# A two-layer streaming encoder step: plain products in the first two SwiGLU pairs, x on a second queue, padded attention tiles, earlier output weights, one root chain

## The chip, the cores and the metric

The kernel runs on one core of a Trainium2 chip. The core has five engines that run side by side, each with its own instruction queue: TensorE (PE, matmuls; its weight loads are listed as PEld), VectorE (DVE), ScalarE (ACT), GpSimd (POOL) and SyncE (SP, which here only issues DMAs). The metric is the device time of one execution in microseconds, as the median of several runs.

## What is computed

560 columns (512 frames of a prompt, 32 frames of a running stream, 16 meta tokens) of width 1024 pass through two layers. Each layer is a half-step SwiGLU, a mixer, and a second half-step SwiGLU; the first layer's mixer is a gated linear attention (GLA), the second's a latent attention (MLA).

```python
def swiglu_half(h, norm_w, w_gate, w_up, w_down):
    hn = rmsnorm(h, norm_w)
    return h + 0.5 * ((jax.nn.silu(hn @ w_gate) * (hn @ w_up)) @ w_down)
...
for i in range(DEPTH):
    hp = swiglu_half(hp, ffn1_norm[i], ...)      # hs (the sample) alike
    xp = rmsnorm(hp, mix_norm[i])
    if i % N_MIXERS == 0: dp, sp = gla_mixer(xp, ...)
    else:                 dp, cp, rp = mla_mixer(xp, ...)
    hp = hp + dp
    hp = swiglu_half(hp, ffn2_norm[i], ...)
y_prompt = rmsnorm(hp[:, N_META:], final_norm)
```

In MLA the score of a query and a key is a product over 128 latent channels (folded into the keys' side by the kernel) plus one over 64 rotary channels.

## The kernel before

**Numbers in two parts.** Every matmul operand is kept as a high part in a reduced-precision 4-byte format and a low part, the rest: `split` (L377) makes the high part by a cast on ACT (L378) and the low part by a subtraction on DVE (L379). A product of two numbers is three matmuls: high by high (L419), weight's low by high (L420), weight's high by low (L422). `mm` (L411) writes these for a list of operand tiles.

**The state.** `h` holds the residual stream, 8 tiles of 128 rows by 560 columns, in two halves of 280 columns.

**A SwiGLU** (`ffn`, L576) takes its 22 gate-and-up tiles in pairs. One pair is a 2 x 2 block product (two tiles, two halves of the input rows, two halves of the columns), and `gate_up` (L476) does it with seven products in place of eight, after Strassen and Winograd. Its operands are b11 and b21 (the first column half, rows 0 to 511 and 512 to 1023, scaled by the norm's weight), b22, and the combinations t4 to t7; its weights are the blocks q0 to q3 and sums of them (`Weights`, L283, with DVE additions at L298). Each of the seven products is 24 matmuls of 280 columns into one of the double banks A, B and C. Between the products `gap` issues pieces of the previous group's down projection (`down`, L558, banks Y) as filling. Weights come by DMA on SP's queue (`quadrant`, L395; L399), the high and low parts of a block by `whole` (L401).

**The norm's factor** is not applied to the operands but after the product: squares are summed over the tiles (`square`), a matmul with ones sums over the rows (L451, three columns for three pieces of a half), DVE refines the inverse root in a chain of small steps (`rsqrt`, L463; L465 to L473), and three transposes spread the result over a bank (L458), from where it is copied to `yn`. One such chain is `roots(half)` (L443); in the first pair of a SwiGLU the first half's chain begins after product t6 and the second half's after t5.

**The start.** For the first SwiGLU the operands are made in the pair itself (`lazy`, `make`, L239): b11 and b21 first, then t6, t5, t7, t4 and b22, each when its product is due, with x arriving by DMAs that alternate with those of the first weights on SP's queue (L1362, L1378, L1381). In the later ones the operands are made piece by piece while the projection before them adds to `h` (`Quads.parts`, L187), and the first weights are loaded and summed at the same place (`ahead`).

**GLA** ends with `wout` (L663): the output projection of two heads at a time. With the second pair of heads each piece is followed by the operands of the next SwiGLU; the four weights are loaded one by one when their first piece is due (L667 to L670), on SP's queue, and split on ACT and DVE.

**MLA** (`attention`, L1072): for eight heads and four blocks of 128 queries, `scores` (L1241) makes three matmuls with the keys, one with the high part of the rotary keys over 128 rows (queries' high and low part stacked, L1254) and one with their low part over 64 rows (L1255). For odd heads the queries' parts lie the other way round. `weigh` (L1281) sums five blocks of values, the last of 64 rows. `sample` (L1118) does the running stream, whose 288 keys fill two blocks of 128 and one of 32 rows. `wout` (L1297) is the output projection, with the next SwiGLU's operands behind each piece as in GLA and its weights loaded one by one.

A scheduler orders the instructions of each engine from this program; each engine then runs its own list in order.

Of the kernel before, what the change touches and what calls it, by code (L numbers as in the profile page):

```python
# [18 lines left out]
P = 128  # L19
# [115 lines left out]
class Quads(Normed):  # L135
# [6 lines left out]
    SETS = (("b11", "b21"), ("t5",), ("t6", "b22", "t7", "t4"))  # L142
# [3 lines left out]
    def __init__(self, net, name, halves, pool, tmp, raws):  # L146
# [5 lines left out]
        self.lazy, self.early, self.finish = False, [], {}  # L152
# [14 lines left out]
    def operand(self, op):  # L167

        if self.lazy and op not in self.made:
            self.make(op)  # L170
        return [self.place(op, i) for i in range(4)]
# [7 lines left out]
    def scaled_parts(self, op, i, m):  # L179

        nc = self.net.nc
        hi, lo = self.place(op, i)
        h, w = self.piece(m, 0), self.weight(m)
        nc.scalar.activation(hi, h, AF.Copy, scale=w)
        nc.vector.scalar_tensor_tensor(lo, h, w, hi.bitcast(F32), op0=ALU.mult, op1=ALU.subtract)

    def parts(self, m, hf):  # L187
# [3 lines left out]
        if hf == 0:  # L191
            self.scaled_parts("b11" if m < 4 else "b21", i, m)
# [6 lines left out]
        else:  # L199
            b12, t5 = self.kept.pop(i)  # L200
            q = self.tmp.tile([P, 4, 280], F32, name="q", tag="q", bufs=1)
            t6, b22, t7, t4 = (q[:, j, :n] for j in range(4))
# [36 lines left out]
    def make(self, op):  # L239
# [3 lines left out]
        t = self.tmp  # L243
        if op in ("b11", "b21"):
            for i in range(4):
                self.scaled_parts(op, i, i + 4 * (op == "b21"))
        for i in range(4):
            b12, t5, b22, t6 = (t[4 * j + i][:, :n] for j in range(4)) if t else (None,) * 4
            if op == "t6":
                nc.scalar.activation(b12, self.piece(i, 1), AF.Copy, scale=self.weight(i))  # L250
                v.scalar_tensor_tensor(t5, self.piece(i, 0), self.weight(i), b12, op0=ALU.mult, op1=ALU.subtract)
                nc.scalar.activation(b22, self.piece(4 + i, 1), AF.Copy, scale=self.weight(4 + i))
                v.scalar_tensor_tensor(t6, t5, -1.0, b22, op0=ALU.mult, op1=ALU.subtract)
                net.split(*self.place("t6", i), t6)
            elif op == "t5":
                net.split(*self.place("t5", i), t5)
            elif op == "t7":
                v.tensor_tensor(b12, b22, b12, op=ALU.subtract)
                net.split(*self.place("t7", i), b12)
            elif op == "t4":  # L260
                v.scalar_tensor_tensor(t6, self.piece(4 + i, 0), self.weight(4 + i), t6, op0=ALU.mult, op1=ALU.add)
                net.split(*self.place("t4", i), t6)
            elif op == "b22":
                net.split(*self.place("b22", i), b22)
        self.made.add(op)

    def roots(self, hf):

        c0, c1 = self.halves[hf]
        if self.lazy:  # L270
            for m in range(ND):
                Normed.square(self, hf)
        self.finish[hf] = self.net.roots(hf, c1 - c0, D)
# [63 lines left out]
class Net:  # L337
    def __init__(self, ctx, tc, a):
# [12 lines left out]
        nc.vector.memset(self.ones, 1.0)  # L351
        self.accs = {}
# [48 lines left out]
    def whole(self, src):  # L401
        hi = self.w.tile([P, 8, P], F32R, name="whi", tag="whi")
        lo = self.w.tile([P, 8, P], F32R, name="wlo", tag="wlo")
        self.split(*(t.rearrange("p a b -> p (a b)") for t in (hi, lo)), src)
# [57 lines left out]

    def rsqrt(self, y, s, vh, t, dim):  # L463
# [3 lines left out]
        for _ in range(3):  # L467
            if y.shape[-1] > 3:
# [7 lines left out]
    def gate_up(self, i, l, f, xs, act, tp, between):  # L476
# [6 lines left out]
        if left is None:  # L483
            left = Weights(self, i, l, f, xs.raws)
            for q in (0, 1):
                left.load(q)
                if xs.early:
                    xs.early.pop(0)()
# [3 lines left out]
        def product(to, op, more=False):  # L492
            if xs.lazy and op in ("b11", "b21"):
                w, x = next(left), xs.operand(op)
            else:
                x, w = xs.operand(op), next(left)
# [40 lines left out]
        if first:  # L537
            xs.roots(0)
# [1051 lines left out]
```

## Time and profile before

| | |
|---|---|
| time, median of 3 runs | 2082.53 us (2082.26 to 2088.39) |
| the profiled execution | 2092.07 us, span 2090.3 us |
| mean granted TensorE clock | 0.984 |
| PE busy | 2029.9 us, 97% of the span, 15290 matmuls |
| DVE busy | 1637.7 us, 78% |
| ACT busy | 1018.8 us, 49% |
| DMA queue of SP and ACT | 173.09 MB, 26.1% of 16 engines' span |

Busy time is the time in which an engine executes instructions; waiting is not counted. Since matmuls overlap, a busy PE may still run slowly: what counts there is the distance from the start of one matmul to the start of the next, and the granted clock (PEclk, 1.00 is full speed). A row of the timeline gives the start, the length, the engine, the source line, the operation with output and input tiles, and in brackets how long the engine had been idle and what released it.

### The profile page before, as it was taken

How to read it: one execution, taken by the hardware profiler on the slowest of the kernel's cores; microseconds unless marked ns; L12 is line 12 of the kernel's file. 1: busy time of each engine (PE TensorE's matmuls, PEld its weight loads, DVE VectorE, ACT ScalarE, POOL GpSimd, SP SyncE). 2: the span in 40 equal slices, each digit the busy share in tenths (PEclk: the TensorE clock that was granted, in tenths of full speed). 3: DMA queues.
4: the chain of work that ended last, by engine and by line, in shares of the span. 5: the costliest groups of instructions: out<-in, count | busy, mean ns of one | idle time of the engine just before them, and what ended most of it. 6: DMA issues, size and time to landing. Idle time of an engine off the chain costs nothing.

```text
span 2090.3 us, 38017 instructions
## 1 busy us (share of the span) xinstructions
PE 2029.9 (97%) x15290; PEld 1985.0 (95%) x15290; DVE 1637.7 (78%) x3097; ACT 1018.8 (49%) x1822; POOL 51.3 (2%) x117
## 2 busy tenths in 40 slices
PE   5999999999998999999999999999999999999997
PEld 5999999989998999999999999999988899999997
DVE  7887879656657987878888878796787898877884
ACT  6444445445535544444455444454575565444451
POOL 0000000101110000000000000000110000000000
PEclk8999999999999999999999999999999999999998
DMA  3233231212222223233312232323111313333221
GB/s 132 87 101 101 83 110 61 96 66 72 66 81 73 65 96 106 83 107 104 101 55 93 86 106 89 101 69 105 60 55 43 126 46 97 101 97 102 86 77 58
DMA packets 91905, 180.16 MB, mean 86 GB/s; under 512 B 10240, under 2 KB 21888, under 8 KB 91728
## 3 DMA queue, kind: packets, MB, share of 16 engines
q1 hardware_dynamic: 87904, 173.09, 26.1%
q10 hardware_dynamic: 3824, 4.63, 0.7%
q8 instruction: 120, 1.97, 0.4%
q14 instruction: 57, 0.47, 0.1%
HBM read 173.69 MB, written 3.99 MB: 85 GB/s over the span
## 4 chain that ended last, share of the span: by engine, by line
PE 81%; DVE 10%; DMA 3%; ACT 2%; issue 2%; SPq 0%; POOL 0%; DVEq 0%; ACTq 0%; POOLq 0%
PE Y L422 8%; PE Y L419 8%; PE Y L420 8%; PE A L420 5%; PE A L422 5%; PE A L419 5%; PE ps L419 3%; PE C L420 3%; PE B L420 3%; PE C L419 3%; PE B L419 3%; PE B L422 3%; PE C L422 3%; PE ps L422 3%; PE ps L420 3%; DVE wlo L379 3%
## 5 line engine op out<-in xcount | busy, mean ns | idle before, releaser
L419 PE MATMUL Y<-ah,whi 128*128 128x280 f32 (+1 forms) x1408 | 376.1, 293 | 6.2 <-ACT ah L378 4.2
L379 DVE TENSOR_TENSOR wlo<-fr,whi 128x1024 fp32r<-128x1024 f32 x308 | 372.0, 1217 | 9.0 <-ACT whi L378 8.6
L420 PE MATMUL Y<-ah,wlo 128*128 128x280 f32 (+1 forms) x1408 | 375.4, 293 | 0.0
L378 ACT CAST whi<-fr 128x1024 fp32r<-128x1024 f32 x308 | 320.5, 1049 | 96.9 <-PE C L422 37.5
L419 PE MATMUL A<-x,whi 128*128 128x280 f32 (+1 forms) x1056 | 283.8, 294 | 16.1 <-ACT whi L378 16.1
L420 PE MATMUL A<-x,wlo 128*128 128x280 f32 (+1 forms) x1056 | 283.4, 294 | 1.0 <-DVE wlo L379 1.0
L419 PEld LDWEIGHTS Y<-ah,whi 128*128 128x128 f32 x1408 | 266.7, 189 | 8.1 <-ACT ah L378 5.1
L570 DVE SCALAR_TENSOR_TENSOR h<-Y,h 128x280 f32<-128x280 f32 (+1 forms) x320 | 140.9, 443 | 162.4 <-PE Y L422 161.7
L420 PEld LDWEIGHTS Y<-ah,wlo 128*128 128x128 f32 x1408 | 266.9, 190 | 0.0
L379 DVE TENSOR_TENSOR wlo<-raw,whi 128x512 fp32r<-128x512 f32 (+5 forms) x231 | 196.0, 850 | 77.6 <-ACT whi L378 72.8
L378 ACT CAST whi<-raw 128x512 fp32r<-128x512 f32 (+5 forms) x231 | 169.8, 736 | 163.4 <-PE ps L422 48.5
L422 PE MATMUL Y<-al,whi 128*128 128x280 f32 (+1 forms) x1408 | 234.4, 292 | 0.0
L298 DVE TENSOR_TENSOR fr<-fr 128x1024 f32<-128x1024 f32 x176 | 214.4, 1218 | 20.5 <-DMA fr<-W 18.7
L419 PEld LDWEIGHTS A<-x,whi 128*128 128x128 f32 x1056 | 201.5, 191 | 16.8 <-ACT whi L378 16.5
L420 PEld LDWEIGHTS A<-x,wlo 128*128 128x128 f32 x1056 | 201.7, 191 | 1.4 <-DVE wlo L379 1.4
L422 PEld LDWEIGHTS Y<-al,whi 128*128 128x128 f32 x1408 | 201.9, 190 | 0.0
L420 PE MATMUL C<-x,wlo 128*128 128x280 f32 (+1 forms) x704 | 189.2, 294 | 3.5 <-DVE wlo L379 3.5
L419 PE MATMUL C<-x,whi 128*128 128x280 f32 (+1 forms) x704 | 189.3, 293 | 0.6 <-ACT whi L378 0.6
L419 PE MATMUL B<-x,whi 128*128 128x280 f32 (+1 forms) x704 | 188.2, 292 | 0.7 <-ACT whi L378 0.7
L420 PE MATMUL B<-x,wlo 128*128 128x280 f32 (+1 forms) x704 | 187.9, 293 | 0.6 <-DVE wlo L379 0.5
L422 PE MATMUL A<-x,whi 128*128 128x280 f32 (+1 forms) x1056 | 180.8, 293 | 0.0
L506 ACT COPY r<-A 128x560 f32<-128x560 f32 (+1 forms) x132 | 82.3, 623 | 171.3 <-PE A L422 170.1
(368 smaller groups left out, 4071.6 us busy)
## 6 DMA issues: line engine op xcount, KB each, us to landing
fr<-W SPq DMA_DIRECT2D x352, 256.0 KB, 3.4
raw<-W SPq DMA_DIRECT2D x80, 512.0 KB, 3.5
raw<-W SPq DMA_DIRECT2D x100, 256.0 KB, 3.0
raw<-W SPq DMA_DIRECT2D x40, 128.0 KB, 2.0
h<-xT SPq DMA_DIRECT2D x3, 560.0 KB, 7.5
raw<-W SPq DMA_DIRECT2D x4, 384.0 KB, 3.1
o_y<-h SPq DMA_DIRECT2D x8, 136.0 KB, 2.7
o_y<-h ACTq DMA_DIRECT2D x8, 136.0 KB, 2.4
```

The source lines that it names most:

```text
L298: self.net.nc.vector.tensor_tensor(r[out], r[x], r[y], op=ALU.add)
L378: self.nc.scalar.copy(hi, src)
L379: self.nc.vector.tensor_tensor(lo, src, hi.bitcast(F32), op=ALU.subtract)
L419: f(hi[:, b0 + k, :], xh[:, c], start=not more and k == 0, stop=False)
L420: f(lo[:, b0 + k, :], xh[:, c], start=False, stop=False)
L422: f(hi[:, b0 + k, :], xl[:, c], start=False, stop=k == n - 1)
L506: nc.scalar.copy(r[:, :, :n], of[:, :, :n])
L570: nc.vector.scalar_tensor_tensor(self.h[:, m, c], Y[:, :n], 0.5, self.h[:, m, c], op0=ALU.mult, op1=ALU.add)
```

## The change

1. **First SwiGLU, first two pairs.** `plain_gate_up` takes the place of `gate_up`: eight plain products with the operands b11, b21, b12 and b22 and the weights q0 to q3, no sums of blocks. The first pair makes its operands as they are due (`direct`) and copies its results out until the norm's factor is there; the second pair makes the combined operands for the later pairs in four of its gaps (`combine`). From the third pair on `gate_up` goes on as before.
2. **Loads.** The norm weights and the first column half of x are issued on ACT's queue; SP's begins with the first weight block. The first weight is split in two halves. A one-column Silu on ones stands ahead of the x loads on ACT, and eleven matmuls on ones (128 x 128) stand ahead of the first product on PE.
3. **One root chain** (`roots2`) for both halves, six columns wide, in the first pair of every SwiGLU, after product t6 (in the first SwiGLU, after the fourth plain product).
4. **Padding in MLA.** The low parts of the rotary keys, the last block of values and of the weights on it, and the third block of the sample's past get zero rows up to 128; the queries' parts lie the same way for all heads.
5. **Early weights.** The four weights of the last output projection of GLA and of MLA are loaded before its first piece.

```diff
+    def plain_gate_up(self, i, l, f, xs, act, tp, between):
...
+        def product(to, q, op, more=False):
+            if early and not more:
+                x = xs.direct(op)
+            if q not in w:
+                w[q] = self.whole(W.r[q], 2 if early and q == 0 else 1)
+            if not early or more:
+                x = xs.direct(op)
+            for j in range(2):
+                self.mm(to[:, j, :n], w[q], 4 * j, x, (0, n), more)
+            if early and q < 2:
+                for _ in range(4):
+                    Normed.square(xs, op[-1] == "2")
...
+        def gap():
+            done[0] += 1
+            if not early and done[0] <= 4:
+                xs.combine(done[0] - 1)
+            if done[0] < 8:
+                between(done[0])
...
+        for (j, hf), bank, tag in zip(((0, 0), (0, 1), (1, 0), (1, 1)), "ACBA", ("ra", "rb", None, None)):
+            D = self.bank2(bank)
+            for kh in (0, 1):
+                product(D, 2 * j + kh, ("b11", "b21", "b12", "b22")[2 * hf + kh], kh == 1)
+                if kh == 0:
+                    gap()
+            held.append((j, hf, hold(D, tag) if tag else D))
+            if early and (j, hf) == (0, 1):
+                xs.roots()
...
     def gate_up(self, i, l, f, xs, act, tp, between):
...
         if first:
-            xs.roots(0)
+            xs.roots()
...
             finish(0, 0, C, r1, ALU.add)
-            xs.roots(1)
...
             def wout(g):
...
+                if g == 1:
+                    for b in (0, 2, 1, 3):
+                        L[b] = self.load(("go", g, b))
...
         def scores(h, t):
...
-                pe.matmul(o, qr[hi, qc], rpl[hi, kc], start=False, stop=True)
+                pe.matmul(o, qr[:, qc], rpl[:, kc], start=False, stop=True)
...
         def weigh(h):
...
-            self.mm3(O[:, 384:512], (vh[:64, 4, hc], vl[:64, 4, hc]), (eh, el), False, False)
+            self.mm3(O[:, 384:512], (vh[:, 4, hc], vl[:, 4, hc]), ee, False, False)
...
                     if heads[-1] == MH - 1:
+                        for b in (0, 2, 1, 3):
+                            W[b] = self.load(("mo", heads[0], b))
                         gone.close()
                         after.append(turn())
...
-    nc.sync.dma_start(net.nv, a["nv"])
+    nc.scalar.dma_start(net.nv, a["nv"])
...
-        nc.sync.dma_start(net.h[:, k0:k1, c0:c1], a["xT"][:, k0:k1, c0:c1])
-
-    x0.lazy = True
-    x0.early = [lambda: x_in(4, 8, 0), lambda: (x_in(0, 4, 1), x_in(4, 8, 1), nc.sync.dma_start(net.ident, a["ident"]))]
+        (nc.scalar if hf == 0 else nc.sync).dma_start(net.h[:, k0:k1, c0:c1], a["xT"][:, k0:k1, c0:c1])
+
+    x0.plain = 2
+    x0.first = Weights(net, 1, 0, 0, x0.raws)
+    x0.first.load(0)
     x_in(0, 2, 0)
     x_in(2, 4, 0)
+    x_in(4, 8, 0)
+    x0.first.load(1)
+    x_in(0, 4, 1)
+    x_in(4, 8, 1)
+    x0.first.load(2, 3)
...
+    warm = net.bank("Y")
+    for _ in range(11):
+        nc.tensor.matmul(warm[:, :P], net.ones, net.ones, start=True, stop=True)
```

ScalarE at the program's start, before (h is the residual stream that x is loaded into, nv the norm weights, fr a weight block as it arrives, whi its high part, x the operands' parts):

```order
L184 ACT_TABLE_LOAD [waits DMAHW1_49]
L184 ACTIVATE x_114<-h_64,nv_65 128x280 [waits DMAHW0_49]
L184 ACTIVATE x_115<-h_64,nv_65 128x280
L184 ACTIVATE x_116<-h_64,nv_65 128x280 [waits DMAHW2_49]
L378 CAST whi_110<-fr_99 128x1024 [waits DMAHW4_49,DMAHW3_49]
L184 ACTIVATE x_117<-h_64,nv_65 128x280
L436 ACTIVATE acc_262<-h_64 128x280
```

The same place on ScalarE, now:

```order
L1459 DMA nv_65<-nv 128x67
L344 ACT_TABLE_LOAD
L344 ACTIVATE silu_69<-ones_67 128x1 [waits DVE_49]
L1475 DMA h_64<-xT 128x2x280 x2
L1475 DMA h_64<-xT 128x4x280 [waits DMAHW0_49]
L181 ACTIVATE x_130<-h_64,nv_65 128x280 [waits DMAHW4_49]
L181 ACTIVATE x_131<-h_64,nv_65 128x280
L181 ACTIVATE x_132<-h_64,nv_65 128x280 [waits DMAHW6_49]
L181 ACTIVATE x_133<-h_64,nv_65 128x280
L371 CAST whi_151<-fr_78 128x512 [waits DMAHW1_49]
L371 CAST whi_151<-fr_78 128x512 [waits DMAHW2_49]
```

The table load now waits for no DMA and stands ahead of the x loads, which ACT itself issues; the weight's cast has become two of half the width, both behind the four operands.

VectorE in GLA's output projection, before (raw is an output weight as it arrives, wlo a weight's low part, q the combined operands of the next SwiGLU, acc its sums of squares, ps the bank of a piece):

```order
L206 SCALAR_TENSOR_TENSOR q_7775<-h_64,nv_65,q_7775 128x280 [waits DVE_49]
L223 TENSOR_TENSOR acc_7676<-acc_7676,sq2_7782 128x280 [waits Activation_49]
L223 TENSOR_TENSOR acc_7678<-acc_7678,sq2_7782 128x280
L379 TENSOR_TENSOR wlo_7796<-raw_7794,whi_7795 128x1024 [waits DMAHW4_49]
L379 TENSOR_TENSOR x_7614<-q_7775,x_7614 128x1120 [waits Activation_49]
L379 TENSOR_TENSOR wlo_7818<-raw_7816,whi_7817 128x1024 [waits DMAHW5_49]
```

The same operands of the next SwiGLU on VectorE, now:

```order
L203 SCALAR_TENSOR_TENSOR q_7782<-h_64,nv_65,q_7782 128x280 [waits DVE_49]
L220 TENSOR_TENSOR acc_7683<-acc_7683,sq2_7789 128x280 [waits Activation_49]
L220 TENSOR_TENSOR acc_7685<-acc_7685,sq2_7789 128x280
L372 TENSOR_TENSOR wlo_7798<-fr_7636,whi_7797 128x1024 [waits DMAHW5_49,DMAHW4_49]
L372 TENSOR_TENSOR x_7627<-q_7782,x_7627 128x1120 [waits Activation_49]
L760 TENSOR_TENSOR h_64<-ps_7801,h_64 128x280 [waits PE_49]
```

The two low parts from raw have left this place (they now stand ahead of the projection, among the last head's rows); that from fr, a weight of the next SwiGLU, stands here now.

TensorE in the first pair of the SwiGLU behind GLA, before (ident and ry are the transposes of the inverse roots, ones and acc the sums that begin a chain):

```order
L422 MATMUL B_8088<-x_7612,whi_8089 128x280
L458 MATMUL Y_8121<-ident_66,ry_8074 128x128 [waits DVE_49]
L458 MATMUL Y_8121<-ident_66,ry_8074 128x128 x2
L451 MATMUL Y_8131<-ones_67,acc_7678 128x1 [waits PE_49]
L451 MATMUL Y_8131<-ones_67,acc_7678 128x1 x2
L419 MATMUL A_7988<-x_7613,whi_8149 128x280 [waits Activation_49]
```

The same place on TensorE, now:

```order
L418 MATMUL A_7983<-x_7629,whi_8129 128x280
L475 MATMUL Y_8119<-ident_66,ry2_8072 128x128 [waits DVE_49]
L475 MATMUL Y_8119<-ident_66,ry2_8072 128x128 x2
L475 MATMUL Y_8161<-ident_66,ry2_8072 128x128 [waits PE_49]
L475 MATMUL Y_8161<-ident_66,ry2_8072 128x128 x2
L415 MATMUL C_8171<-x_7626,whi_8172 128x280
```

Both halves' transposes now follow one another, one product later than the first half's did, and the sums of the second half have moved up to those of the first.

More of the change, by code (lines that the diff above doesn't have):

```diff
@@ L151, in __init__ @@
         self.sets, self.kept, self.made = None, {}, set()
-        self.lazy, self.early, self.finish = False, [], {}
+        self.plain, self.finish = 0, {}
     def place(self, op, i):
@@ L237, in __call__, with direct, combine @@
             self.first.sums()
-    def make(self, op):
+    def direct(self, op):
+        m0, hf = {"b11": (0, 0), "b21": (4, 0), "b12": (0, 1), "b22": (4, 1)}[op]
+        pairs = [(t[:, 0, :self.n], t[:, 1, :self.n]) for t in self.extra] if op == "b12" else self.operand(op)
+        if op not in self.made:
+            self.made.add(op)
+            for i, (hi, lo) in enumerate(pairs):
+                self.scaled_parts(hi, lo, m0 + i, hf)
+        return pairs
+    def combine(self, i):
         net, nc, n = self.net, self.net.nc, self.n
@@ L242, in make @@
         v = nc.vector
[L243 to L273, printed above, removed]
+        f, g, q = self.tmp[i % 2], self.tmp[2], self.tmp[3]
+        b12, b22, t5, t4, t6, t7 = f[:, 0, :n], f[:, 1, :n], g[:, 0, :n], g[:, 1, :n], q[:, 0, :n], q[:, 1, :n]
+        for x, m in ((b12, i), (b22, 4 + i)):
+            nc.scalar.activation(x, self.piece(m, 1), AF.Copy, scale=self.weight(m))
@@ L461, in roots, with roots2, finish @@
         return finish
+    def roots2(self, n, dim):
+        pe = self.nc.tensor
+        s = self.bank("s")
+        first = (0, P, n - P)
+        for hf in (0, 1):
+            for j, c in enumerate(first):
+                k = 3 * hf + j
+                pe.matmul(s[:, k:k + 1], self.accs[hf][:, c:c + P], self.ones[:, :1], start=True, stop=True)
+        y, vh, t = (self.np_.tile([P, 6], F32, name=x, tag=x) for x in ("ry2", "rv2", "rt2"))
+        self.rsqrt(y, s[:, :6], vh, t, dim)
+        def finish(hf):
+            out = self.bank("s")
+            for j in (2, 0, 1):
+                k = 3 * hf + j
+                pe.transpose(out[:, first[j]:first[j] + P], y[:, k:k + 1].to_broadcast([P, P]), self.ident)
+            return out[:, :n]
+        return [partial(finish, hf) for hf in (0, 1)]
     def rsqrt(self, y, s, vh, t, dim):
@@ L484, in gate_up @@
             left = Weights(self, i, l, f, xs.raws)
[L485 to L488, printed above, removed]
+            left.load(0, 1)
         left = iter(left)
@@ L492, in product @@
         def product(to, op, more=False):
[L493 to L496, printed above, removed]
+            x, w = xs.operand(op), next(left)
             for j in range(2):
@@ L556, in gate_up, with finish, hold @@
         gap()
+    def plain_gate_up(self, i, l, f, xs, act, tp, between):
+        nc = self.nc
+        v = nc.vector
+        n = xs.n
+        early = xs.plain == 2
+        W, w = xs.first, {}
+        xs.first = None
+        if W is None:
+            W = Weights(self, i, l, f, xs.raws)
+            W.load(0, 1, 2, 3)
+        def product(to, q, op, more=False):
[10 more added lines that the diff above has]
+                    Normed.square(xs, op[-1] == "2")
+        def finish(j, hf, src):
+            gu = tp.tile([P, 2, 280], F32, name="gu", tag="gu", bufs=2)
+            t = gu[:, :, :n]
+            y = xs.scale(hf).unsqueeze(1).to_broadcast([P, 2, n])
+            v.tensor_tensor(t, src[:, :, :n], y, op=ALU.mult)
+            g, u = gu[:, 0, :n], gu[:, 1, :n]
+            nc.scalar.activation(g, g, AF.Silu)
+            v.tensor_tensor(g, g, u, op=ALU.mult)
+            c = slice(*xs.halves[hf])
+            self.split(act[j][0][:, c], act[j][1][:, c], g)
+        def hold(of, tag):
+            if not early:
+                return of
+            r = tp.tile([P, 2, 280], F32, name="r", tag=tag, bufs=1)
+            nc.scalar.copy(r[:, :, :n], of[:, :, :n])
+            return r
+        done = [0]
+        def gap():
[4 more added lines that the diff above has]
+                between(done[0])
+        held = []
+        for (j, hf), bank, tag in zip(((0, 0), (0, 1), (1, 0), (1, 1)), "ACBA", ("ra", "rb", None, None)):
[7 more added lines that the diff above has]
+                xs.roots()
+            if not early or j:
+                for x in held:
+                    finish(*x)
+                held = []
+            gap()
+        xs.plain -= 1
```

115 lines of the change are left out of this document (69 added, 46 removed).

## The prediction

> **What bounds the kernel now.** I read the page first, then the clock and the engines' busy time by stretches of the program, then the timelines of the stretches that lose. The first row of the page:
>
> ```profile
> PE 2029.9 (97%) x15290; PEld 1985.0 (95%) x15290; DVE 1637.7 (78%) x3097; ACT 1018.8 (49%) x1822; POOL 51.3 (2%) x117
> ```
>
> The matmul engine (PE) is busy for 97% of the span. Only two things can then move the time: the number of matmuls, and the places where PE waits or runs slowly. The view of busy time by stretches (stretch, length, busy us of each engine with its instruction count, granted clock PEclk, DMA share) says where those places are:
>
> ```profile
> core 0: us, PE busy (x) PEld busy (x) DVE busy (x) ACT busy (x) POOL busy (x), PEclk, DMA share, GB/s
> 0.00:64.00 64.00, 39.51 (x200) 37.37 (x201) 48.23 (x110) 36.73 (x76) 0.20 (x4) 0.79 0.36 118
> 64.00:360.00 296.00, 296.00 (x2298) 296.00 (x2297) 245.30 (x354) 140.27 (x216) 0.00 (x0) 1.00 0.28 90
> 657.00:707.00 50.00, 42.70 (x312) 41.55 (x312) 45.16 (x95) 30.97 (x50) 0.00 (x0) 0.93 0.28 90
> 1505.00:1660.00 155.00, 152.29 (x1019) 134.52 (x1019) 126.89 (x394) 99.16 (x273) 15.65 (x38) 1.00 0.21 61
> 1660.00:1677.00 17.00, 17.00 (x120) 15.89 (x120) 14.73 (x33) 7.02 (x18) 0.00 (x0) 1.00 0.47 165
> 1677.00:1713.00 36.00, 33.37 (x244) 32.13 (x243) 34.03 (x72) 24.50 (x39) 0.00 (x0) 0.95 0.10 31
> ```
>
> The second row is the steady state: 296.0 us / 2298 = 0.1288 us a matmul, with no gap, at full clock. Against that pitch the start loses most: 200 matmuls x 0.1288 = 25.8 us of work fill 64 us, so 38.2 us are lost. GLA's output projection (657 to 707) and MLA's (1677 to 1713) lose a few us each; there VectorE (DVE) is busy for 90% and 95%. MLA's attention (1505 to 1660) hardly idles, yet it issues one matmul in 155/1019 = 0.152 us, above the steady pitch. The rest of the span is untouched by the change: its matmuls and their order stay.
>
> **The start.** PE's own timeline shows its largest waits there (start, length, instruction, in brackets the idle time before it and what ended it):
>
> ```profile
> 9.10 0.60 PE L419 MATMUL A<-x,whi 128*128 128x280 f32 x1 [9.10 <-ACT whi L378]
> ...
> 25.20 0.60 PE L419 MATMUL A<-x,whi 128*128 128x280 f32 x1 [6.43 <-ACT whi L378]
> ...
> 37.47 0.54 PE L458 MATMUL Y<-ident,ry 128*128 128x128 f32 x3 [1.37 <-DVE ry L473]
> ...
> 47.30 0.60 PE L420 MATMUL C<-x,wlo 128*128 128x280 f32 x1 [3.49 <-DVE wlo L379]
> ```
>
> Nothing can start before 9.10. The 6.43 us are the wait for the third product's weight: a sum of blocks, which DVE makes after it has made all Strassen operands of the first pair. The 1.37 us are the root chain, the 3.49 us again a summed weight. Two neighbouring stretches show what such a gap does to the clock:
>
> ```profile
> 35.60:38.80 3.20, 1.61 (x13) 1.29 (x12) 3.20 (x12) 2.09 (x6) 0.00 (x0) 1.00 0.00 0
> 39.00:42.20 3.20, 3.20 (x14) 3.20 (x15) 3.03 (x12) 2.35 (x5) 0.00 (x0) 0.50 0.50 161
> ```
>
> With PE busy for only 1.61 of 3.20 us at full clock, the next stretch is granted half: 14 matmuls in 3.20 us, 0.229 each.
>
> The change removes the sums and the four combined operands from the first pair, and pays with one product more in each of two pairs. A product has 24 matmuls, so it adds 48 x 0.1288 = 6.2 us of PE work. The 200 become 248, or 31.9 us. What remains lost is the arrival of the first operand, the half clock after it, and late operands. For the arrival:
>
> ```profile
> 4.32 1.28 ACT L184 ACT_TABLE_LOAD   x1 [4.32 <-DMA h<-xT]
> ...
> 8.00 1.04 ACT L378 CAST whi<-fr 128x1024 fp32r<-128x1024 f32 x1 [1.02 <-DMA fr<-W]
> ...
> 16.23 1.78 ACT L252 ACTIVATE xt<-h,nv 128x280 f32<-128x280 f32 x4
> fr<-W SPq DMA_DIRECT2D x18, 256.0 KB, 4.2
> h<-xT SPq DMA_DIRECT2D x3, 560.0 KB, 7.5
> h<-xT SPq DMA_DIRECT2D x2, 280.0 KB, 3.4
> ```
>
> The last three rows are DMA issues with their median time to landing. On ScalarE's (ACT's) queue the norm weights and the table load (1.28) go first, so x is issued at about 2.6 and lands about 3.4 later, at 6.0 to 6.5. The weight, now first on SyncE's (SP's) queue, has landed by then. Four scaled operands take 1.78 and half of a weight's cast about half of 1.04, so the first matmul comes at 8.6 (estimate). It runs after an idle time far beyond the one above, so the first product runs at half clock: 24 x (0.229 - 0.129) = 2.4. That the table is loaded before x lands takes it off this path; the matmuls on ones end before the first operand exists and cost nothing but idle PE time. After that ACT is next: in the first four products it makes 16 scaled operands (4 x 1.78 = 7.1) and four casts (4.2), and the squares, in the 4 x 3.1 us that PE needs. I leave 1.6 us for waits behind it and for the root chain, which now has two products of plain work in front of its transposes. Sum: 31.9 + 8.6 + 2.4 + 1.6 = 44.5 against 64, a gain of **19.5**. Lower bound: arrival as before (9.1), half clock (2.4) and one wait as large as the largest of before with a second of 1 us (7.4), 64 - 50.8 = 13.2. Upper bound: arrival at 8.2 and nothing else, 64 - 40.1 = 23.9. I take the value nearer to the upper end, since the sums behind 6.43 and 3.49 have left the path.
>
> A rule speaks to the matmuls on ones. The Trainium skill (TensorE: Matmul & The Clock Gate, What's actually happening) has the full clock come after a busy window of about 3.4 us and go after one idle window of that length; by it, if no window lay wholly idle between the ones and the first product, that product would run at full speed and the time would be 2.4 lower than mine. The trace's pair of stretches above, where half a window of idle time was enough, speaks against it, and I keep the 2.4.
>
> **GLA's output projection.** DVE decides there: rows of both engines.
>
> ```profile
> 675.68 1.22 DVE L379 TENSOR_TENSOR wlo<-raw,whi 128x1024 fp32r<-128x1024 f32 x1
> ...
> 676.95 0.60 PE L420 MATMUL ps<-o,wlo 128*128 128x280 f32 x1 [5.24 <-DVE wlo L379]
> ...
> 720.11 0.54 PE L458 MATMUL Y<-ident,ry 128*128 128x128 f32 x3 [2.54 <-DVE ry L473]
> ```
>
> PE waits 5.24 us for a weight's low part, which stands on DVE behind the next FFN's operands. The early loads take two such splits (one after another about 1.14 each, 2.3 together) out of this stretch. Since DVE is its bound (45.16 of 50), the stretch gets shorter by those 2.3 and not by 5.24: what PE waits for next is the residual sums and operands that stand in the same DVE row. The cover of the moved splits is the heads before, where PE has no gap. The single root chain has both halves' transposes once; of the 2.54 wait of the second chain I take 2.2, since one chain of six columns remains. Gain **4.5**; bounds 0 (operands take the freed time) and 7.8 (5.24 + 2.54). In the other FFNs no wait of this kind stands at the chain, so one chain less is worth nothing there.
>
> **The padding.** PE's timeline of the attention:
>
> ```profile
> 1523.84 0.29 PE L428 MATMUL s<-kl,x 128*128 128x272 f32 x1
> 1523.96 0.29 PE L1254 MATMUL s<-rph,x 128*128 128x272 f32 x1
> 1524.18 0.39 PE L1255 MATMUL s<-rpl,x 64*128 64x272 f32 x1
> 1524.50 0.39 PE L426 MATMUL s<-kh,x 128*128 128x256 f32 x1
> 1524.72 0.28 PE L427 MATMUL s<-kh,x 128*128 128x256 f32 x1
> ```
>
> Between full-height matmuls of 272 columns the step is 0.12 (23.84 to 23.96). The 64-row one starts 0.22 after the last of them, the next 0.32 later, and the one after that 0.22: 0.76 for three steps that would take 3 x 0.12 to 0.125 = 0.37, so 0.39 lost. How many there are:
>
> ```profile
> L1255 PEld LDWEIGHTS s<-rpl,x 64*128 64x128 f32 x40 | 7.3, 183 | 6.2 <-issue 3.0
> ```
>
> By the code, 14 more stretches of 64- or 32-row matmuls (eight of the last values block, four of the sample's past, two of its scores) bring the count to 54, so at most 54 x 0.39 = 21.1. What is late next is DVE: the padded layout adds one operation per rotation of the queries, 8 x 0.44 by the width of its operands, so DVE has 126.89 + 3.5 = 130.4 us of work in 155 - 21.1 = 133.9 us, 97%. The GLA stretch above managed 90% with gaps. If that is the limit, the attention takes 130.4/0.903 = 144.4 and the gain is 10.6. I take **14.4**, with which DVE is busy for 130.4/140.6 = 93%, between the 90% and the 95% of the two stretches above; bounds 10.6 and 21.1. The zero fills go to GpSimd (15.65 busy of 155) and to DVE before the attention, where PE does not wait for them: nothing.
>
> Here a rule speaks against the change. The Trainium skill (TensorE: Matmul & The Clock Gate, Why this matters for your kernels) holds that a single matmul of 32 rows takes the same time as one of 128; by that the padding would bring nothing of its own. The steps of 0.22, 0.32 and 0.22 against 0.12 contradict it where heights alternate, and I go by them.
>
> **MLA's output projection.** Two more splits of this kind:
>
> ```profile
> 1687.22 1.21 DVE L379 TENSOR_TENSOR wlo<-raw,whi 128x1024 fp32r<-128x1024 f32 x1
> ...
> 1692.16 1.22 DVE L379 TENSOR_TENSOR wlo<-raw,whi 128x1024 fp32r<-128x1024 f32 x1
> ```
>
> They leave a stretch where DVE is busy for 34.03 of 36 us: 2.3, and up to 36 - 244 x 0.1288 = 4.6 if all of PE's loss goes. Their cover is thin: in the 17 us before, DVE has 14.73, and with 2.3 more it is full. I take **3.2**, bounds 0 and 4.6.
>
> **Sum.** 19.5 + 4.5 + 14.4 + 3.2 = 41.6. The profiled execution took 2092.07 us (span 2090.3), 0.5% above the median of the runs, 2082.53. By the profile the changed kernel takes 2050.5; as a median 2082.53 - 41.6 = **2040.9**.
>
> **Rivals.**
> *DVE bounds the attention.* If the eight operations and the closer spacing leave PE waiting wherever it gained, the padding gives 5 instead of 14.4: 2050. For it speaks the 97% it would need at most; against it, that the steady FFN stretch runs DVE at 245.30/296 = 83% without one gap. Chance 0.10.
> *The start is paced by ACT or by the loads.* All of x and eight half blocks of weights come at once, and ACT has more work per product than before. If a wait of 6 us comes back, and half clock once more with it, the start gives about 8: 2052. Chance 0.08.
> *The padding does not do what it says.* If the long steps come from the change of operands and banks there, not from the height, the 14.4 go: 2055. The Trainium skill's rule on 32-row matmuls would give this time. Against it stands that the other full-height matmuls between the same banks show no such step. Chance 0.05.
> *Slower, by the clock.* Place: the two plain pairs with their fill pieces, 444 matmuls, where the operands of both pairs are made while PE consumes them. If PE idles half of each 3.4 us there, as at 35.6, each matmul costs 0.10 more. It decides from 41.6/0.10 = 416 such matmuls on; with all 444 and the first two products of the third pair (492) the time is 2041 + 49 = 2090. For it: half clock for part of the start before (0.79 in the mean). Against it: plain operands need two operations instead of a chain, and the two largest gaps inside the first pair, 9.9 us, came from sums that are gone. Chance 0.02.
>
> **The numbers.** My forecast has 0.74, the rivals 0.10, 0.08, 0.05 and 0.02, a change within the noise 0.01. A measurement of this kernel can tell 0.3%, 6.2 us, from no change. All cases but the last two are faster by more than that: faster 0.97, within 0.3% 0.015, slower 0.015. All lower bounds together give 13.2 + 0 + 10.6 + 0 = 23.8, a time of 2058.7; all upper ones 23.9 + 7.8 + 21.1 + 4.6 = 57.4, 2025.1. All ends at once are unlikely, but the rivals lie at 2050 to 2055: the range is 2030 to 2057.
>
> **What would show it.** In the changed profile: the first product at 8 to 9 us at half clock; the 64-us stretch's work (248 matmuls) done by about 44.5; no wait above 2 us for a weight in the first pair; steps of 0.12 at the rope's low part, and DVE above 90% in the attention; no DVE row of a raw weight in the output projections. Wrong would be: gaps of several us in the first two pairs with ACT as the releaser, an attention still of 150 us, or a stretch elsewhere, between 64 and 360 above all, that lost its even pitch.

## The result and the profile after

The changed kernel takes 2054.55 us as a median (2050.96 to 2056.61, 4 runs); the kernel before, beside it, 2082.4 (2079.64 to 2088.39, 4 runs). The ratio is 0.9853, interval 0.9831 to 0.9874. The forecast was 2040.9 with a range of 2030 to 2057: faster, and inside the range, but 31 us faster by the ratio (2082.4 x 0.0147), 27.9 by the two medians, and not 42. The time alone is also the 2055 of the rival that the padding does nothing; the length of the attention, below, decides against that rival.

Busy time by stretches of the changed kernel, cut where the same matmuls stand as in the stretches 0 to 64, 64 to 360, 657 to 707 and 1677 to 1713 of before:

```profile
core 0: us, PE busy (x) PEld busy (x) DVE busy (x) ACT busy (x) POOL busy (x), PEclk, DMA share, GB/s
0.00:42.90 42.90, 38.39 (x270) 37.78 (x271) 33.73 (x80) 31.76 (x71) 0.20 (x4) 0.96 0.62 213
42.90:339.20 296.30, 296.14 (x2299) 295.88 (x2298) 240.38 (x352) 136.57 (x211) 0.00 (x0) 1.00 0.27 85
633.40:682.80 49.40, 43.54 (x311) 42.86 (x311) 46.29 (x91) 29.39 (x48) 0.00 (x0) 0.93 0.27 88
1640.40:1675.70 35.30, 32.02 (x244) 31.80 (x243) 32.55 (x68) 23.89 (x38) 0.00 (x0) 0.95 0.01 1
```

The start's 64 us became 42.9, with 70 PE instructions more. The two output projections are about as full on DVE as before, 94% (90% before) and 92% (95%), and 0.6 and 0.7 us shorter.

The traces hold 15290 and 15360 matmuls; the 70 are 22 records of the ones and the 48 new ones, all ahead of the third pair. So the n-th matmul from the end is the same work in both, but for some neighbours that changed places, and the time between two such matmuls can be set side by side. The marks are those of the first profile of before; the numbers are differences of start times:

```
from..to (us, before)  0..64  64..410  410..480  655..740  1510..1665  1665..1735
before                  63.9    346.1      70.1      85.0       155.0        69.9
before, again           60.4    347.2      71.6      81.7       156.4        71.2
changed                 42.9    346.1      67.7      80.9       144.1        71.6
```

The start gained 17 to 21 us, the attention 11 to 12, GLA's output projection with the pair behind it (655 to 740) 1 to 4, MLA's nothing (it took 0.4 to 1.7 more). Between 64 and 410 nothing moved. The GLA heads (410 to 480) came out 2 to 4 us shorter, which the prediction did not have; that stretch has waits of 0.4 to 1.2 us with half a clock behind some of them, and takes 66.9 to 72.4 us in the fourteen profiles of this document.

PE's timeline at the start, after:

```profile
1.05 5.05 PE L1513 MATMUL Y<-ones 128*128 128x128 f32 x22 [1.05 <-DVE ones L343]
9.44 0.60 PE L415 MATMUL A<-x,whi 128*128 128x280 f32 x1 [3.34 <-ACT whi L371]
...
12.85 0.29 PE L415 MATMUL A<-x,whi 128*128 128x280 f32 x1
...
33.55 0.82 PE L475 MATMUL Y<-ident,ry 128*128 128x128 f32 x6
```

The row at 12.85 is where the full clock returns, half a product after its beginning. The waits of 6.43, 3.49 and 1.37 have no successor: the transposes at 33.55 found the roots ready.

The attention, after, at the rope's low part:

```profile
1496.13 0.28 PE L424 MATMUL s<-kl,x 128*128 128x272 f32 x1
1496.25 0.29 PE L1349 MATMUL s<-rph,x 128*128 128x272 f32 x1
1496.37 0.29 PE L1350 MATMUL s<-rpl,x 128*128 128x272 f32 x1
1496.50 0.28 PE L422 MATMUL s<-kh,x 128*128 128x256 f32 x1
1496.61 0.28 PE L423 MATMUL s<-kh,x 128*128 128x256 f32 x1
```

Steps of 0.12, 0.13 and 0.11 where 0.22, 0.32 and 0.22 stood.

### The profile page after: what moved, and what is told of

It is laid out like the page before. It is cut to its first block, busy times and chain, and to the rows that moved or that the text cites. A ratio compares the mean times of both kernels' runs of the same rounds, so it can differ in the third digit from the quotient of the medians.

```text
span 2053.1 us, 38088 instructions
## 1 busy us (share of the span) xinstructions
PE 2006.6 (98%) x15360; PEld 1975.7 (96%) x15360; DVE 1619.7 (79%) x3044; ACT 1009.5 (49%) x1811; POOL 52.6 (3%) x121
## 4 chain that ended last, share of the span: by engine, by line
PE 79%; DVE 13%; DMA 4%; ACT 2%; issue 2%; SPq 0%; POOL 0%; DVEq 0%; ACTq 0%; POOLq 0%
PE Y L418 8%; PE Y L415 8%; PE Y L416 8%; PE A L416 5%; PE A L415 5%; PE A L418 5%; DVE wlo L372 4%; PE ps L415 3%; PE B L416 3%; PE B L418 3%; PE B L415 3%; PE C L418 3%; PE C L416 3%; PE C L415 3%; PE ps L418 3%; PE ps L416 3%
## 5 line engine op out<-in xcount | busy, mean ns | idle before, releaser
L372 DVE TENSOR_TENSOR wlo<-fr,whi 128x1024 fp32r<-128x1024 f32 (+1 forms) x303 | 365.2, 1215 | 9.6 <-ACT whi L371 9.3
L371 ACT CAST whi<-fr 128x1024 fp32r<-128x1024 f32 (+1 forms) x303 | 314.9, 1048 | 101.6 <-PE C L418 40.6
L415 PE MATMUL A<-x,whi 128*128 128x280 f32 (+1 forms) x1056 | 281.6, 292 | 3.6 <-ACT whi L371 3.3
L290 DVE TENSOR_TENSOR fr<-fr 128x1024 f32<-128x1024 f32 x168 | 204.9, 1220 | 25.0 <-DMA fr<-W 22.8
L415 PE MATMUL C<-x,whi 128*128 128x280 f32 (+1 forms) x688 | 181.9, 290 | 0.0
L416 PE MATMUL C<-x,wlo 128*128 128x280 f32 (+1 forms) x688 | 181.8, 290 | 0.0
L418 PE MATMUL A<-x,whi 128*128 128x280 f32 (+1 forms) x1056 | 178.3, 291 | 0.0
L517 ACT COPY r<-A 128x560 f32<-128x560 f32 (+1 forms) x126 | 78.4, 623 | 165.4 <-PE A L418 163.7
```

What stands on the lines that cost most here:

```text
L290: self.net.nc.vector.tensor_tensor(r[out], r[x], r[y], op=ALU.add)
L371: self.nc.scalar.copy(hi, src)
L372: self.nc.vector.tensor_tensor(lo, src, hi.bitcast(F32), op=ALU.subtract)
L415: f(hi[:, b0 + k, :], xh[:, c], start=not more and k == 0, stop=False)
L416: f(lo[:, b0 + k, :], xh[:, c], start=False, stop=False)
L418: f(hi[:, b0 + k, :], xl[:, c], start=False, stop=k == n - 1)
```

## The experiments

All times are medians beside runs of the kernel before on the same chip.

**A second profile of before.** No edit.

> The kernel before, unchanged, for a second profile: its first one took 2092.07 us where the median of its runs is 2082.4. If the 9.7 us between them are spread over places that the change does not touch, a second profile ends 5 to 12 us earlier, and the difference sits in the clock after gaps (start, GLA heads). If they belong to the start, where waits are long, the difference sits in the first 92 us. The attention is expected to take the same 155 us within 0.5 in both theories.

2087.11 us (one run), its span 2085.3: 5 us less than the first profile. The start is 3.5 shorter, the stretch 655 to 740 3.3; the attention took 1.4 more. The attention had been expected within 0.5, and neither expectation, all in the start or all elsewhere, came out alone. So one profile of this kernel places each stretch that has gaps only to some 3 us, and the first profile lay at the upper end.

**Only the loads.** The kernel before with the start of the changed one, Strassen products kept:

```diff
-    nc.sync.dma_start(net.nv, a["nv"])
+    nc.scalar.dma_start(net.nv, a["nv"])
...
+    x0.first = Weights(net, 1, 0, 0, x0.raws)
+    x0.first.load(0)
```

> The kernel before with only the change to the loads: norm weights and the first half of x on ACT's queue, the table load and the matmuls on ones ahead, the first weight ahead on SP's queue; the first pair still has seven products with sums. Theory (the plain products made the start's gain): the wait for the summed weight stays, and the point that the kernel before reaches at 92 us comes within 3 us of it, so the time is within 4 us of the kernel before. Rival (the loads made it): that point comes 8 us or more earlier, the plain products gave the rest.

Ratio 1.0006 (0.9993 to 1.0019). Its PE timeline:

```profile
6.78 0.39 PE L420 MATMUL A<-x,whi 128*128 128x280 f32 x1 [0.97 <-ACT x L184]
...
23.96 0.60 PE L420 MATMUL A<-x,whi 128*128 128x280 f32 x1 [7.45 <-ACT whi L379]
```

The first product began 2.3 us earlier than before. In front of the first summed weight the wait grew from 6.43 to 7.45, and the product behind it began 1.2 earlier (23.96 against 25.20). At the 64-us mark the kernel stood at 62.6, between the two profiles of before (63.9 and 60.4): nothing was left of the lead that can be told from them. With the plain products on top the start gets shorter; the plain products without the new loads were not run.

**The padding undone.**

```diff
...
-                pe.matmul(o, qr[:, qc], rpl[:, kc], start=False, stop=True)
+                pe.matmul(o, qr[hi, qc], rpl[hi, kc], start=False, stop=True)
...
```

> The changed kernel with the padding of the attention undone (the early weights stay). Theory (matmuls of alternating height cost about 0.39 us each, and DVE's throughput keeps back half of it): the attention takes 155 us again in place of 144, about 11 us more than the changed kernel, with the steps of 0.22 and 0.32 back. Rival (the attention got faster by something else, such as its place in the clock's windows): it stays within 3 us of 144.

Ratio to before 0.989 (0.9869 to 0.9911), a median of 2062.6. Attention of the three kernels, from the same matmul to the same matmul; no padding first, then the changed one:

```profile
1478.00:1633.60 155.60, 152.56 (x1013) 134.41 (x1012) 127.11 (x390) 99.36 (x275) 15.01 (x38) 1.00 0.22 66
```

```profile
1482.00:1626.10 144.10, 136.46 (x1012) 129.73 (x1012) 130.25 (x398) 98.31 (x275) 14.91 (x38) 1.00 0.23 68
```

Without padding 155.6 us, as before, and its timeline has the old steps (1492.45 to 1492.67 to 1492.98 to 1493.21). PE's busy time fell by 152.6 - 136.5 = 16.1 with the padding; its idle time rose from 3.0 to 7.6. That is the answer to where the rest went: 11.5 = 16.1 - 4.6.

**Why the idle time rose.** DVE is busy for 130.25 of 144.10 us, 90%, which is what the lower bound of the prediction had assumed as DVE's limit. Two kernels take 32 operations of 0.39 us, 12.5 us, from DVE there; its busy time in the attention fell by 9.6 and 8.9. The first moves the division to ACT:

```diff
-        nc.vector.tensor_scalar(p[:, :n], p[:, :n], st[:, 5:6], None, op0=ALU.mult)
+        nc.scalar.activation(p[:, :n], p[:, :n], AF.Copy, scale=st[:, 5:6])
```

> The changed kernel with one DVE operation of the softmax moved to ACT (the division by the sum as an activation with a scale: 32 operations, 12.5 us of DVE's 129.2 in the attention); ACT has 98 us of work in these 144. Theory (DVE's throughput is the bound of the padded attention): the attention shrinks from 144 to about 137, where PE without gaps would be, so 5 to 8 us less in the time. Rival (the waits come from the latency of the softmax's chain, not from how much DVE does): 144 within 2 us, or more, since the chain now crosses to ACT's queue.

Ratio 0.9853 (0.9829 to 0.9876). The attention got longer:

```profile
1481.20:1628.00 146.80, 137.83 (x1013) 131.41 (x1011) 120.61 (x364) 113.70 (x308) 15.46 (x38) 0.99 0.22 68
```

The second leaves the division out:

```diff
-        nc.vector.tensor_scalar(p[:, :n], p[:, :n], st[:, 5:6], None, op0=ALU.mult)
```

> The changed kernel without the division of the attention weights by their sum (that part of the softmax is left out, 32 operations of 0.39 us on DVE, 12.5 us; nothing takes its place on another engine). It tells apart what moving the division to ACT left open. Theory now (what keeps PE waiting in the padded attention is the chain from one operation to the next at a few places, not the sum of DVE's work): the attention stays within 3 us of 144 although DVE has only 118 us of work in it. Rival (DVE's throughput, and in the run before ACT's work took back the gain): it falls to 138 or less.

Ratio 0.9846 (0.9827 to 0.9865), attention:

```profile
1482.20:1625.90 143.70, 135.94 (x1012) 129.82 (x1011) 121.40 (x364) 98.39 (x275) 15.33 (x38) 1.00 0.23 69
```

DVE at 84% and no extra work on ACT: still 143.7. The theory that DVE's throughput bounds the padded attention falls. What is left are single waits of 0.4 to 1.8 us for one result each (low parts of the values and of the transposed weights, steps of the softmax). With the division left out there are still 1.8 for the values, 1.5 for the transposed weights and 1.3 for the softmax's exponentials on ACT. That they come because PE gets there sooner is argued; which of them could be taken away was not tried.

**The early weights undone.**

```diff
...
-                        for b in (0, 2, 1, 3):
-                            W[b] = self.load(("mo", heads[0], b))
```

> The changed kernel with the early loads of the last output weights of GLA and MLA undone. The prediction's theory (two splits of 1.14 us leave DVE's full stretch): GLA's projection gets 2.3 us longer again, MLA's 2 to 3. Rival (the row that the two splits leave is taken at once by two splits of the next SwiGLU's weights, so DVE's work in the stretch stays as it was): both within 1 us of the changed kernel.

Ratio 0.9854 (0.9826 to 0.9881): no difference in the time. In GLA the stretch 655 to 740 took 81.3 (80.9 with early weights), within 1 us as the rival had it; in MLA 1665 to 1735 took 68.9 (71.6), shorter, which neither had. In GLA the wait of 5.24 us for a low part is back with late weights; early ones put two waits of 3.30 and 2.43 for residual additions in its place. What DVE does in MLA's projection shows why nothing was gained; of before (1677 to 1713), and of the changed kernel (1638.5 to 1676.1):

```profile
L379 DVE TENSOR_TENSOR wlo<-fr,whi 128x1024 fp32r<-128x1024 f32 x3 | 3.6, 1212 | 0.0
...
L379 DVE TENSOR_TENSOR wlo<-raw,whi 128x1024 fp32r<-128x1024 f32 x2 | 2.4, 1214 | 0.0
```

```profile
L372 DVE TENSOR_TENSOR wlo<-fr,whi 128x1024 fp32r<-128x1024 f32 x5 | 6.1, 1217 | 0.0
```

Two splits of output weights left, and two of the next SwiGLU's weights took their place: before, those two began at 1663.8 and 1672.8, ahead of the stretch, where the early weights now are. (The fifth one begins at 1675.78, at the end of the second window.) PE's wait moved to the residual additions; PE and DVE of the changed kernel:

```profile
1658.06 0.60 PE L415 MATMUL ps<-x,whi 128*128 128x272 f32 x1 [3.28 <-DVE h L1412]
```

```profile
1655.23 1.22 DVE L372 TENSOR_TENSOR wlo<-fr,whi 128x1024 fp32r<-128x1024 f32 x1
1656.37 1.28 DVE L372 TENSOR_TENSOR x<-q,x 128x1088 fp32r<-128x1088 f32 x1
1657.57 1.13 DVE L1412 TENSOR_TENSOR h<-ps,h 128x272 f32<-128x272 f32 x3
```

Three pieces fill the three banks; the first addition that frees one stands behind a weight's split and an operand's. That MLA is better off with late weights is not shown by its 2.7 us alone: with early ones the stretch took 69.4 to 72.7 in seven profiles (that with squares on POOL left out), with late ones 68.7 to 71.2 in five, and 71.5 in the kernel with spare banks below.

**Squares on POOL.**

```diff
...
-                nc.vector.tensor_tensor(acc, acc, sq[:, a:b], op=ALU.add)
+                nc.gpsimd.tensor_tensor(acc, acc, sq[:, a:b], op=ALU.add)
```

> The changed kernel with the sums of squares of the later SwiGLUs' inputs (16 additions per projection, about 0.38 us each, 6 us) on POOL in place of DVE. Theory (in the two output projections DVE's row is full and the residual additions, for which PE waits, stand behind the operands in it): the waits of 3.3 and 2.4 us in GLA's and of 3.3 us in MLA's projection shrink by 2 to 4 us each, 4 to 8 us in the time. Rival (the waits come from the order of the rows, the three residual additions behind a large split, whatever else DVE does): less than 1.5 us each.

Ratio 0.9892 (0.9869 to 0.9915), 8 us worse than the changed kernel; neither theory had that. On POOL one addition costs

```profile
L220 POOL TENSOR_TENSOR acc<-acc,sq 128x272 f32<-128x272 f32 x14 | 14.6, 1060 | 14.6 <-ACT sq L213 14.6
```

1.06 us in place of 0.43 on DVE, and the stretch 1665 to 1735 grew by 5.7. GLA's stretch 655 to 740 stayed within 0.2. DVE has 16 operations less in it, 125 and not 141, but its busy time there did not fall, 73.0 us against 73.2: other operations of DVE got longer. Three of its rows there, with the squares on POOL and in the changed kernel:

```profile
L372 DVE TENSOR_TENSOR x<-t,x 128x280 fp32r<-128x280 f32 x4 | 3.2, 804 | 0.1
L203 DVE SCALAR_TENSOR_TENSOR q<-h,nv,q 128x280 f32<-128x280 f32 x4 | 3.1, 766 | 0.0
L201 DVE SCALAR_TENSOR_TENSOR q<-t,q 128x280 f32<-128x280 f32 x4 | 2.9, 734 | 0.0
```

```profile
L372 DVE TENSOR_TENSOR x<-t,x 128x280 fp32r<-128x280 f32 x4 | 1.8, 446 | 0.0
L203 DVE SCALAR_TENSOR_TENSOR q<-h,nv,q 128x280 f32<-128x280 f32 x4 | 2.0, 506 | 0.0
L201 DVE SCALAR_TENSOR_TENSOR q<-t,q 128x280 f32<-128x280 f32 x4 | 1.8, 444 | 0.0
```

So this run took nothing off DVE, and says nothing on whether DVE's sum bounds the projections.

**Two chains again.**

```diff
-            xs.roots()
+            xs.root(0)
...
+            xs.root(1)
```

> The changed kernel with two root chains again in the first Strassen pair of each later SwiGLU; the first SwiGLU keeps one. Theory (the second chain's wait of 2.54 us behind GLA is what the single chain saves): between the end of GLA's projection and the pair after it 2 to 3 us come back, elsewhere nothing, 2 to 3 us in the time. Rival (that wait came from the order of the pair in this place in the kernel before, and is gone for another reason): within 0.5 us.

Ratio 0.9888 (0.9855 to 0.9922). The stretch 655 to 740 took 84.2 against 80.9, with a wait of 2.04 for the roots. But of four profiles with two chains it took 85.0 and 84.2 in two, 81.7 and 82.0 in the others: the wait comes and goes, and the single chain takes that risk away, 0 to 3 us. The expectation of nothing elsewhere failed: in later pairs PE waited 1.9 and 2.3 us in front of summed weights (0.8 and 1.0 in the changed kernel), and the stretch 740 to 1510 took 775.3 against 770.1; why was not traced.

**The first product.** x's second pair of tiles on SP's queue; and the ones left out:

```diff
-        (nc.scalar if hf == 0 else nc.sync).dma_start(net.h[:, k0:k1, c0:c1], a["xT"][:, k0:k1, c0:c1])
+        (nc.scalar if hf == 0 and k0 != 2 else nc.sync).dma_start(net.h[:, k0:k1, c0:c1], a["xT"][:, k0:k1, c0:c1])
```

```diff
-    for _ in range(11):
-        nc.tensor.matmul(warm[:, :P], net.ones, net.ones, start=True, stop=True)
```

> The changed kernel with the second pair of x tiles of the first half on SP's queue, ahead of the second weight, in place of ACT's; nothing else moves. In the changed kernel those two tiles land at 7.9 us, since the second weight's 512 KB come at the same time, and the first product starts at 9.44. Theory (what bounds the start now is the order in which 1.1 MB land, not ACT): the first product starts 1 to 2 us earlier and the time falls by 1 to 2 us. Rival (ACT's four operands and the half casts, or the DMA engines' common rate, set it): within 0.5 us.

> The changed kernel without the eleven matmuls on ones. Prediction's step (idle before the first product halves its clock, with or without the ones): the first product starts at the same 9.4 and no later one is slower, within 0.5 us; where the window falls otherwise, the whole first product at half clock, at most 1.5 us more. Rival (the ones shorten the half-clock stretch): 1.5 us or more come on top at the first product, and nothing after it.

Ratios 0.9841 (0.9824 to 0.9857) and 0.9832 (0.9817 to 0.9848): neither differs from the changed kernel in the time. With x on both queues the first product began at 8.61, 0.83 earlier, and the mark at 64 us (before) came at 42.93, where the changed kernel has 42.89: the full clock returned 1.0 us later and took it back. Without the ones the product ran at half clock to its end; its PE timeline

```profile
15.04 1.14 PE L418 MATMUL A<-x,whi 128*128 128x280 f32 x4
15.97 0.39 PE L415 MATMUL A<-x,whi 128*128 128x280 f32 x1
16.19 0.30 PE L416 MATMUL A<-x,wlo 128*128 128x280 f32 x1
```

reaches full pitch only at 16.2, and the mark comes 1.6 us later, 0.3 of which is a first product that began at 9.71. That is at the border of the two expectations, and it is not shown to be the work of the ones. The kernel with squares on POOL has the same start with the same eleven ones; its PE timeline:

```profile
9.50 0.60 PE L415 MATMUL A<-x,whi 128*128 128x280 f32 x1 [3.62 <-ACT whi L371]
...
15.76 0.29 PE L415 MATMUL A<-x,whi 128*128 128x280 f32 x1
```

Half clock for 6.3 us, as without the ones. In the eight profiles with the changed kernel's start it lasted 3.3 to 6.3 us and the mark came at 42.9 to 44.8; in the three profiles without ones (two of them of before) it lasted 5.1 to 6.5. The clock that the traces record changes at points 3.41 us, or a multiple of it, apart. In the changed kernel these are 5.95, 9.36 and 12.78: the first product began 0.08 us behind the second point and had full clock from the third. With squares on POOL they are 5.51, 8.92 and 15.75: it began 0.58 behind the second, and half clock lasted over two steps of 3.41. All fourteen starts fit this reading, that the place of these points decides and not the ones; no run moves the points alone.

**Spare banks.** Late weights in MLA, and the second halves' pieces of both last projections in the banks for scores:

```diff
-                    Y = self.bank()
+                    Y = self.bank("s" if g == 1 and hf else "ps")
...
```

> The changed kernel with MLA's output weights loaded late again (2.7 us shorter at that place in the run before) and with the second halves' pieces of both last output projections in the five banks that the mixers use for scores, idle there, so that eight pieces and not three can stand before DVE adds them. Theory (PE waits for a bank that DVE frees late, because three additions stand behind a weight's split and an operand's): the waits of 2 to 5 us in both projections go, and 2 to 4 us of the time with them. Rival (DVE is full, 44 of 47 us, and only the place of the wait moves, to the operands of the next SwiGLU): less than 1 us beyond the 2.7.

Ratio 0.9835 (0.9818 to 0.9852). GLA's stretch fell from 80.9 to 78.4 (78.5 in the next kernel, which has these banks too; 80.8 to 81.7 in the seven profiles with early weights, one chain and three banks). MLA's took 71.5, so the theory holds for GLA alone. There a wait of 6.17 us now stands in front of the first product of the next SwiGLU: PE ran ahead and waits once.

**What was left, together.** x on both queues, fifteen matmuls on ones, GLA's spare banks, MLA's late weights.

> The changed kernel with what the runs before leave: the second pair of x tiles on SP's queue, fifteen matmuls on ones in place of eleven (at 0.43 us each they end at about 7.5, one us before the first product), the second halves' pieces of GLA's last projection in the banks for scores, MLA's output weights loaded late. Theory (the gain of 0.83 at the first product was lost to the half clock, which ended later; without an idle window ahead of it the product runs at full clock): the first product starts at 8.6 with a pitch of 0.13, the point that the changed kernel reaches at 42 us comes 1.5 to 2 us earlier, GLA's projection is 2.5 us shorter, MLA's 1.5; about 2049 us, 0.25 to 0.3% below the changed kernel. Rival (the stages after a gap take what phase the clock's windows give them, and small edits are not added up): within 2 us of the changed kernel's 2054.55.

2047.66 us, ratio 0.9828 (0.9811 to 0.9845), the fastest kernel here. Against the changed kernel's 0.9853 that is 0.25% less, with intervals that still overlap. The stretches: start 41.9 (42.9), 655 to 740 78.5 (80.9), 1665 to 1735 69.1 (71.6). The first product came at 8.09 and, against the theory, still ran at half clock from its third matmul on:

```profile
1.05 5.75 PE L1511 MATMUL Y<-ones 128*128 128x128 f32 x30 [1.05 <-DVE ones L343]
8.09 0.39 PE L415 MATMUL A<-x,whi 128*128 128x280 f32 x1 [1.29 <-ACT whi L371]
8.81 0.48 PE L416 MATMUL A<-x,wlo 128*128 128x280 f32 x1 [0.33 <-DVE wlo L372]
9.09 0.44 PE L415 MATMUL A<-x,whi 128*128 128x280 f32 x1
```

Idle times of 1.29 us ahead of it and 0.33 behind its first matmul were enough for that: in the 3.41 us up to 8.97, where the clock halved, PE was busy for 1.79.

## Why the prediction was right, and where it was too high

*The start, 19.5.* Right in size and cause: 21.0 by the first profiles, 17.5 against the second one. The loads alone gave nothing that the time shows, as the step assumed in putting the gain on the sums. The first product came at 9.44 and not 8.6: the second pair of x landed only at 7.9, beside the second weight. The half clock lasted for half of the product and cost 1.2 rather than 2.4 (12 matmuls up to 12.85, 0.10 each), and the waits behind it were almost none. That the half clock was so short was luck: of the eight profiles with this start the changed kernel's reached the mark first, at 42.9, the last at 44.8, where the gain is 15.6 to 19.1.

*The clock.* The Trainium skill (TensorE: Matmul & The Clock Gate, What's actually happening) was set against the trace with the ones. Its first half, that a busy window releases the clock, is what the start shows: from 9.36 to 12.78 PE was busy for 3.22 us, and the full clock came. Its second half, one whole idle window before the clock halves, the last kernel does not show: idle times of 1.29 and 0.33 us were followed by half clock.

*The padding, 14.4.* The mechanism is right, the size was off: 11.5, near the lower bound of 10.6. The matmuls gave 16.1 and not 21.1: the step priced one place at 0.39 and took that for all 54, which came to 0.30 on average. And 4.6 came back as waits, where the step had left room for 6.7 (21.1 - 14.4). The bound's reason, DVE's throughput, was wrong: without the division DVE had 84% and the attention the same length. The rival that the padding does nothing is refuted: 155.6 against 144.1. The rule of the Trainium skill (TensorE: Matmul & The Clock Gate, Why this matters for your kernels) on single matmuls of few rows does not hold where heights alternate.

*GLA's output projection, 4.5, and MLA's, 3.2.* Here the step failed that read "they leave a stretch". The splits left, and the scheduler filled DVE's row again: in MLA with two splits that before stood ahead of the stretch, in GLA with a split and a sum of weights that stood behind it. The rows of the order shown with the change had it: a low part from fr stands where two from raw stood. Of the 4.5 the chain's part is real in some runs; of the 2.3 of the splits late weights give back 0.4, and MLA's 3.2 did not come: its stretch took 0.4 to 1.7 us more than before.

*The base.* The sum was subtracted from the median, but its terms were read from a profile that was 9.7 us slower than the median. Its start was 3.5 us longer than that of the second profile and its stretch 655 to 740 3.3, so gains read from it are too large by as much, set against a median. The spans fit this: the changed kernel's profile is 37.2 us shorter than the first profile of before, 32.2 shorter than the second, and the medians are 27.9 apart.

## What to carry to other kernels

When instructions are moved out of a stretch where an engine is full, look in the new order at what moves in: the gain is the change of that engine's sum there, not the price of what left. An engine at 90% beside a waiting one is not thereby its bound: take work off it, see that its busy time fell, and see whether the stretch moves. Read the waits of at least two profiles before pricing them, since those that meet a clock's window or a transfer's arrival change by microseconds from run to run. An effect at such a place, as that of the ones, is not settled by one profile with it and one without.

## What the runs showed of the hardware

POOL adds two tiles of 128 x 272 in 1.06 us where DVE takes 0.43, and in the stretch where it did so three kinds of DVE's operations on tiles of 128 x 280 took 0.73 to 0.80 us where they take 0.44 to 0.51 otherwise. A matmul of 64 rows between ones of 128 lengthens the steps around it to 0.22 and 0.32 where 0.12 is usual; zero rows up to 128 take all of that away. Eleven 128 x 128 matmuls on ones show as 22 records 0.21 us apart; full clock came 3.3 to 6.3 us after the first product's start with them and 5.1 to 6.5 us without. x in two transfers of 280 KB took 5.2 us to land beside the weights on the other queue, 3.4 us when they shared one queue and came first:

```profile
h<-xT ACTq DMA_DIRECT2D x2, 280.0 KB, 5.2
```
